# Key and query norms of a DeltaNet head in one logarithm, exponents formed once for all heads, bf16 row parts from one transpose

## The chip, the core and the metric

One core of a Trainium2 chip runs the whole program. The metric is the device time of one execution in microseconds; the time before is the median of three runs.

## The reference

A two-layer hybrid backbone over 1280 tokens (256 of context, 1024 latents on a 16 x 64 grid), width 1024. Layer 0 mixes with an mLSTM beside an S5 scan, layer 1 with a bidirectional gated DeltaNet of 8 heads of 128; each is followed by a SwiGLU network. The change lies in layer 1 alone. Cut to that:

```python
qkv = silu(depthwise_conv3x3(h @ w_in[:, :3 * 1024], conv_w))     # context: one row
q, k = l2norm(q) * 128 ** -0.5, l2norm(k)                         # per head and token
for r in (forward, backward):
    g = -exp(a_log[r]) * softplus(a_pre + dt_bias[r]);  beta = sigmoid(b_pre)
    # in chunks of 128 tokens, G = cumsum(g), Gt = its last value
    gamma = exp(G[i] - G[j]) where i >= j
    A     = strict lower of (k beta) k^T * gamma;   solve (I + A) [U, W] = [v beta, k beta exp(G)]
    attn  = q k^T * gamma;   qg = q exp(G);   kd = k exp(Gt - G)
    S     = exp(Gt) S + kd^T (U - W S);   o = qg S + attn (U - W S)
y = rmsnorm(o) * silu(z) @ w_out
```

## The kernel before

Large products run on TensorE (PE) in three parts of reduced precision (`mm3`, L116 to L118: high by high, high by low, low by high). The weights of a block come from DRAM by SP's queue; ScalarE (ACT) makes the high part (L109), GpSimd (POOL) subtracts for the low part (L110).

The projection stage of layer 1 runs over eight heads (`gdn_project`). For a head it computes keys, queries, the output gate (heads 0 to 5 here, `LATE = 6`) and values. A `conv_block` is a product in pieces of 256 and 512 tokens into PSUM, an ACT copy into a padded image (L1650, row of context L1647), the first tap on ACT (L1665, L1672), eight more taps on VectorE (DVE; L1669, each 128x1024) with two for the context row (L1674), and the silu as tanh on ACT (L1679) and a product on DVE (L1680).

Between these pieces stands a generator of side work, `gdn_keys(h)`, which is started before the values of its own head and ends during the next head. `pull` takes one piece of it halfway through each product and one after; the counts of its `yield`s (`Y1` to `Y5` = 6, 2, 1, 1, 2) set how many pieces lie between its steps. The steps are: the keys are transposed to token order (`to_tokens`, `tt_ps`, L1689) with sums of squares on ACT (L1697); the logarithm of the norms, a polynomial of small DVE operations (`log_half`, L1522 to L1536); the exponents `d_ei`, `d_ej`, `d_dx` from it and from the gates' cumulative sums `G` (L1755 to L1761); a transpose of the row exponent, `d_pr` (L1768); its split into three bf16 parts, `rows` (L1772 to L1777), which are multiplied with a selector `sel3` to spread a row over partitions (`d_pE`, L1802; `d_pe`, L1817); the queries' transposes and logarithm (L1790, L1793); the queries times their decay (POOL, L1806); and, in three groups of chunks, the decay matrices `d_e` (ACT, L1820), their sum on POOL (L1828), the key products `d_pk` (L1825) with `d_ca` (DVE, L1829), and the query products `d_pq` (L1837, DVE L1840).

PE executes in the order of the program text (`in_pe_order`). The order on DVE, ACT and POOL is set by a scheduler that models the engines; the steps of the generator carry a raised priority (`HP = 400`). After heads 3 and 6, the triangular base inverses of three heads (`gdn_base`: `b_t`, `b_x`, L1877 to L1890) are added on DVE and POOL, and the scheduler spreads them over the heads that follow. Head 7 starts its generator ahead of its queries (`last`).

Of the kernel before, what the change touches and what calls it, by code (L numbers as in the profile page):

```python
# [41 lines left out]
class Kernel:  # L42
# [77 lines left out]
    def dense(self, w, rhs, kb, n, c0=0, order=None, mid=0):  # L120
        """Feature-major product: psum[m, t] = sum_k w[k, m] act[k, t]; rhs(k) gives the two parts.
        mid: pieces of side work halfway."""
        ps = self.psd.tile([P, 512], F32, name="pd")
# [4 lines left out]
        return ps[:, :n]

    # ---------------------------------------------------------------- conditioning  # L130
    def cond_vectors(self, cp):
# [107 lines left out]
    def norm_sums(self, key, n):  # L239
        """Column sums of squares -> psum [128, n/128]."""  # L240
# [6 lines left out]
    def acts(self, ci):  # L247
        """The two parts of a chunk's activations, one after another in the same place."""
# [34 lines left out]
    # Pieces of work that follow one another while the tensor engine goes on with something else.  # L283
# [16 lines left out]
    # ---------------------------------------------------------------- program  # L300
# [43 lines left out]
    # ---------------------------------------------------------------- layer 0: mLSTM  # L344
# [26 lines left out]
    def even_select(self, c):  # L371
        """sel[p, (r, h), m] = 1 where p is row 32 r + h or 64 + 32 r + h."""
# [11 lines left out]
    def onehot(self, out, row):  # L384
        """out[p, m] = 1 where p == row."""
# [5 lines left out]
    def shift_chunks(self, dst, src, r):  # L391
        """dst[chunk] = src[previous chunk in scan order] (first chunk: 0); dims [p, c, ...]."""
# [10 lines left out]
    def mlstm_gate_rows(self, hs, gp):  # L403
        """Gate projections with their biases, a gate kind and direction to each quarter of the partitions."""
# [23 lines left out]
    def mlstm_gates(self, gk):  # L428
        """Decays, stabilisers and the factors that follow from them, in 9 pieces."""
# [12 lines left out]
        # log-sigmoid of the forget gates, order [r, c, h]  # L442
# [21 lines left out]
        # rows 32 r + h  # L464
# [35 lines left out]
        # -m in three bf16 parts: rows 0 to 63 and 64 to 127 of the first tile, rows 0 to 63 of the second  # L500
# [60 lines left out]
    def mlstm_states(self, h, t, dp, wp):  # L561
        """Scaled keys, values and the states entering each chunk, in 12 pieces."""
# [31 lines left out]
    def mlstm_weights(self, g, t, u, sp):  # L594
        """Decayed scores of a group of chunks, both directions, in 3 pieces."""
# [25 lines left out]
    def mlstm_heads(self, g, t, u, sp):  # L621
        """Normalised outputs of a group of chunks, token-major, in k + 1 pieces."""
# [38 lines left out]
    def mlstm_finish(self, g, t, u):  # L661
        """Gated outputs of a group of chunks, feature-major, in one piece."""
# [6 lines left out]
        # (tanh(o/2) + 1) * y; the factor 0.5 * head norm weight follows with the split  # L669
# [5 lines left out]
    def mlstm_outputs(self, dp, wp, sp):  # L675
        """All heads; the stages of a group of chunks lie a step apart, the states come a head ahead."""
# [38 lines left out]
    def emit(self, *streams):  # L715
        """Emit streams (generator, number of pieces), spread evenly among one another."""
# [18 lines left out]
    def run_pieces(self, *streams):  # L735
        """Emit the merged streams, the tensor engine in just this order."""
# [5 lines left out]
    def merge(streams):  # L742
        """One stream of several (generator, number of pieces), spread evenly among one another."""
# [998 lines left out]
    def gdn_keys(self, h, kqv, pool, qp):  # L1742
# [21 lines left out]
        for _ in range(Y1):  # L1764
            yield
# [567 lines left out]
```

## Time and profile before

| | us |
|---|---|
| median of three runs (lowest, highest) | 3623.36 (3621.87, 3625.25) |
| span of the profiled execution | 3623.4 |
| PE busy in the span | 3363.9 (93%) |
| DVE busy | 1981.7 (55%) |
| ACT busy | 996.8 (28%) |
| POOL busy | 1017.9 (28%) |
| projection stage of layer 1, profile time | 1850 to 2450 |

The profiled execution's own time is its span; the runs shown stand within 2 us of it. Busy time leaves out register, branch and semaphore instructions. Line numbers are those of the kernel before.

### The profile page before, as it was taken

Reading aid. Unit: us, or ns where it says so; the run is one execution under the profiler, and the core shown is the slowest. Engines: PE = TensorE matmul, PEld = TensorE weight load, DVE = VectorE, ACT = ScalarE, POOL = GpSimd, SP = SyncE. Lnnn points to the kernel's source line nnn. Section 1 sums busy time; section 2 is a strip of 40 time slices with the busy share of each in tenths; the row PEclk is TensorE's granted clock in tenths of the full one; section 3 lists DMA queues with packets and bytes.
Section 4 is the critical chain, followed back from the end, with each engine's and each line's share of the span. In section 5 each row is a group of like instructions: output and inputs, shape, how many; then the busy total and the mean of one; then the engine's idle time right before and its main releaser. Section 6 shows DMA issues by size and latency. Waiting matters only on the chain.

```text
span 3623.4 us, 48228 instructions
## 1 busy us (share of the span) xinstructions
PE 3363.9 (93%) x18527; PEld 2791.9 (77%) x18527; DVE 1981.7 (55%) x4038; ACT 996.8 (28%) x2375; POOL 1017.9 (28%) x783
## 2 busy tenths in 40 slices
PE   6998988999999999999988979778898999999999
PEld 3787767887777778888877768568897788888888
DVE  7659977434333333333489899995755432222224
ACT  3221135331111111111244535433444211111112
POOL 1011124140111111111344373644543222222123
PEclk7999989999999999999999989889999999999999
DMA  7553575512222221111123424246453011111111
GB/s 239 122 175 122 170 212 148 178 59 83 88 77 79 82 77 58 35 41 36 58 75 95 125 87 132 89 125 211 153 184 133 25 44 53 49 48 49 44 53 65
DMA packets 396828, 360.31 MB, mean 99 GB/s; under 512 B 104763, under 2 KB 329755, under 8 KB 396086
## 3 DMA queue, kind: packets, MB, share of 16 engines
q1 hardware_dynamic: 396598, 357.23, 32.3%
q8 instruction: 146, 2.39, 0.3%
q14 instruction: 84, 0.69, 0.1%
HBM read 258.92 MB, written 96.75 MB: 98 GB/s over the span
## 4 chain that ended last, share of the span: by engine, by line
PE 66%; DVE 23%; DMA 5%; issue 3%; ACT 2%; POOL 1%; SPq 1%; DVEq 0%; POOLq 0%; ACTq 0%
PE pd L116 19%; PE pd L118 18%; PE pd L117 18%; DVE d_fT L1669 4%; DVE d_qT L1669 2%; PE a_ps L181 1%; DVE s_t L1067 1%; DVE bst L1070 1%; DVE s_t L1069 1%; DVE b_x L1883 1%; DVE s_t L1068 1%; DVE b_t L1877 1%; PE e_pk L2030 1%; PE e_pu L2038 1%; DVE hl L268 1%
## 5 line engine op out<-in xcount | busy, mean ns | idle before, releaser
L116 PE MATMUL pd<-hh,w_hi 128*128 128x512 f32 (+1 forms) x3064 | 1148.8, 375 | 2.0 <-ACT hh L276 2.0
L117 PE MATMUL pd<-hl,w_hi 128*128 128x512 f32 (+1 forms) x3064 | 1134.9, 370 | 3.3 <-DVE hl L268 3.1
L118 PE MATMUL pd<-hh,w_lo 128*128 128x512 f32 (+1 forms) x3064 | 1128.2, 370 | 1.6 <-POOL w_lo L110 1.5
L110 POOL TENSOR_TENSOR w_lo<-w_raw,w_hi 128x1024 fp32r<-128x1024 f32 (+2 forms) x205 | 485.3, 2368 | 2056.8 <-ACT w_hi L109 1939.6
L116 PEld LDWEIGHTS pd<-hh,w_hi 128*128 128x128 f32 x3064 | 587.7, 192 | 114.8 <-issue 8.9
L118 PEld LDWEIGHTS pd<-hh,w_lo 128*128 128x128 f32 x3064 | 585.8, 191 | 106.4 <-issue 2.9
L117 PEld LDWEIGHTS pd<-hl,w_hi 128*128 128x128 f32 x3064 | 587.0, 192 | 103.0 <-DVE hl L268 6.1
L109 ACT CAST w_hi<-w_raw 128x1024 fp32r<-128x1024 f32 (+2 forms) x205 | 207.4, 1012 | 1012.8 <-PE pd L117 796.2
L1329 DVE SCALAR_TENSOR_TENSOR x<-pd,mod,x 128x512 f32<-128x512 f32 (+1 forms) x408 | 267.6, 670 | 267.2 <-PE pd L118 266.9
L1317 DVE TENSOR_TENSOR ntmp<-ntmp,pd 128x512 f32<-128x512 f32 (+1 forms) x110 | 69.8, 634 | 509.0 <-PE pd L118 508.8
L116 PE MATMUL pd<-g_hi,w_hi 128*128 128x512 f32 (+1 forms) x844 | 314.8, 373 | 0.6 <-DVE x L1329 0.6
L117 PE MATMUL pd<-g_lo,w_hi 128*128 128x512 f32 (+1 forms) x844 | 307.8, 365 | 0.0
L118 PE MATMUL pd<-g_hi,w_lo 128*128 128x512 f32 (+1 forms) x844 | 303.0, 365 | 0.6 <-POOL w_lo L110 0.6
L1316 DVE SCALAR_TENSOR_TENSOR ntmp<-ntmp,pd 128x512 f32<-128x512 f32 (+1 forms) x110 | 69.7, 634 | 269.9 <-ACT ntmp L1315 268.2
L1669 DVE SCALAR_TENSOR_TENSOR d_fT<-img,wcv,d_fT 128x1024 f32<-128x1024 f32 x128 | 193.7, 1513 | 22.6 <-ACT d_fT L1665 21.5
L116 PEld LDWEIGHTS pd<-g_hi,w_hi 128*128 128x128 f32 x844 | 159.5, 189 | 49.0 <-issue 21.8
L1318 ACT ACTIVATE g_hi<-ntmp 128x512 fp32r<-128x512 f32 (+1 forms) x110 | 64.7, 588 | 442.7 <-DVE ntmp L1317 442.3
L118 PEld LDWEIGHTS pd<-g_hi,w_lo 128*128 128x128 f32 x844 | 158.8, 189 | 28.9 <-issue 2.1
L117 PEld LDWEIGHTS pd<-g_lo,w_hi 128*128 128x128 f32 x844 | 159.7, 189 | 23.2
L1319 DVE SCALAR_TENSOR_TENSOR g_lo<-ntmp,g_hi 128x512 fp32r<-128x512 f32 (+1 forms) x110 | 139.6, 1269 | 68.2 <-ACT g_hi L1318 68.2
L237 POOL TENSOR_TENSOR nacc<-nacc,ntmp 128x256 f32<-128x256 f32 (+1 forms) x72 | 75.1, 1047 | 123.2 <-ACT ntmp L233 121.6
L181 PE MATMUL a_ps<-a_raw,svec 128*32 128x256 f32 x768 | 83.2, 428 | 17.9 <-DMA a_raw<-in_ada_w_dram 17.8
(550 smaller groups left out, 4767.2 us busy)
## 6 DMA issues: line engine op xcount, KB each, us to landing
w_raw<-in_ffn_w_dram SPq DMA_DIRECT2D x106, 512.0 KB
a_raw<-in_ada_w_dram SPq DMA_DIRECT2D x96, 512.0 KB
w_raw<-in_od_w_in_dram SPq DMA_DIRECT2D x32, 512.0 KB
w_raw<-in_ffn_w_dram SPq DMA_DIRECT2D x32, 384.0 KB
w_raw<-in_ev_w_in_dram SPq DMA_DIRECT2D x20, 512.0 KB
x_dr<-x SPq DMA_DIRECT2D x4, 2048.0 KB
p_dr<-mp_t SPq DMA_DIRECT2D x32, 256.0 KB
x<-x_dr SPq DMA_DIRECT2D x16, 512.0 KB
```

Of the source, the lines that this page charges most:

```text
L109: nc.scalar.copy(out=hi, in_=raw)
L110: self.w_lo_engine.tensor_tensor(out=lo, in0=raw, in1=hi.bitcast(F32), op=ALU.subtract)
L116: mm(ps, lh, rh, start=first, stop=False)
L117: mm(ps, lh, rl, start=False, stop=False)
L118: mm(ps, ll, rh, start=False, stop=last)
L181: nc.tensor.matmul(ps[32 * j:32 * j + 32, :256], self.svec[:, k], raw[:, j * 256:(j + 1) * 256], start=(k == 0), stop=(k == KB - 1), tile_ ...
L237: nc.gpsimd.tensor_tensor(out=acc, in0=acc, in1=sq, op=ALU.add)
L1316: nc.vector.scalar_tensor_tensor(out=th[:, :n], in0=th[:, :n], scalar=1.0, in1=p1, op0=ALU.add, op1=ALU.mult)
L1317: nc.vector.tensor_tensor(out=th[:, :n], in0=th[:, :n], in1=p3, op=ALU.mult)
L1319: nc.vector.scalar_tensor_tensor(out=gl[:, t0:t0 + n], in0=th[:, :n], scalar=0.5, in1=gh[:, t0:t0 + n].bitcast(F32), op0=ALU.mult, op1=ALU ...
L1329: nc.vector.scalar_tensor_tensor(out=xd, in0=ps, scalar=g, in1=xd, op0=ALU.mult, op1=ALU.add)
L1669: nc.vector.scalar_tensor_tensor(out=al, in0=g[:, dy:dy + 16, dx:dx + 64], scalar=wc(i), in1=al, op0=ALU.mult, op1=ALU.add)
```

## The change

Per head, the keys' and queries' squares go into one tile of 18 columns, with one logarithm over both; head 7, whose queries come later, takes the two separately. For this the query transposes are issued one `yield` after the key transposes, and the yields ahead of `d_pr` become one fewer. The three exponents per head are formed by one addition of 60 columns to a table `gpre`, which is made once for all heads in `gdn_gates`; the exponentials for `dg_E` and `dg_D` become one ACT operation. The row exponent is copied by ACT to three places of a zeroed 128-column tile, so that one 128x128 transpose brings it to partitions 0, 64 and 96, where the three bf16 parts are made from PSUM with four DVE operations; the selector's blocks move to the same partitions.

```diff
 # log_half(out, x, add, pool, width): its tiles are [P, width], cut to the columns of x
 # sel3: blocks at partitions 0, 64, 96 and no longer 0, 32, 64
 # gdn_gates
+        gED = gk.tile([P, 8, 2, 2, NCH], F32, name="dg_ED")
+        self.gE, self.gD = gED[:, :, 0], gED[:, :, 1]
+        self.gpre = gk.tile([P, 8, 3, 2, NCH], F32, name="dg_pre")
+        col, row, end = (self.gpre[:, :, a].rearrange("p h r c -> p r c h") for a in (0, 1, 2))
+        for r in range(2):
+            nc.vector.tensor_tensor(out=col[:, r], in0=self.lnb[:, r], in1=self.gcum[:, r], op=ALU.subtract)
+            nc.scalar.copy(out=row[:, r], in_=self.gcum[:, r])
+            nc.vector.tensor_tensor(out=end[:, r], in0=col[:, r], in1=self.gtot[:, r], op=ALU.add)
 # gdn_keys
+        def logs(sl):
+            nc.vector.tensor_scalar(out=ssq[:, sl], in0=ssq[:, sl], scalar1=0.25, scalar2=EPS, op0=ALU.mult, op1=ALU.add)
+            self.log_half(lkq[:, sl], ssq[:, sl], -0.6931471805599453, pool, NQ)
+        def factors():
+            lkb = lkq[:, ks].unsqueeze(1)
+            nc.vector.tensor_tensor(out=e3.rearrange("p a r c -> p (a r) c"), in0=self.gpre[:, h].rearrange("p a r c -> p (a r) c"),
+                                    in1=lkb.to_broadcast([P, 6, NCH]), op=ALU.add)
+            for o, n in ((0, 1), (64, 2)):
+                nc.scalar.copy(out=ei3[:, o:o + 32 * n].rearrange("p (b x) -> p b x", x=32)[:, :, :20],
+                               in_=e3[:, 1].rearrange("p r c -> p (r c)").unsqueeze(1).to_broadcast([P, n, 20]))
+            nc.scalar.activation(out=self.gED[:, h], in_=e3[:, 1:3], func=AF.Exp)
+        together = kqv[1] is not None
         with self.tc.high_priority(offset=HP):
-            self.to_tokens(kT, NCH, self.kt_dr[h], ssq, qp)
-            nc.vector.tensor_tensor(out=ej, in0=self.lnb[:, :, :, h], in1=G, op=ALU.subtract)
-            nc.vector.tensor_scalar(out=ssq, in0=ssq, scalar1=0.25, scalar2=EPS, op0=ALU.mult, op1=ALU.add)
-            self.log_half(lk, ssq, -0.6931471805599453, pool, [P, NCH])
-            nc.vector.tensor_tensor(out=ei, in0=G, in1=lkb, op=ALU.add)
-            nc.vector.tensor_tensor(out=ej, in0=ej, in1=lkb, op=ALU.add)
-            nc.vector.tensor_tensor(out=dx, in0=ej, in1=Gt, op=ALU.add)
-            nc.scalar.activation(out=self.gE[:, h], in_=ei, func=AF.Exp)
-            nc.scalar.activation(out=self.gD[:, h], in_=dx, func=AF.Exp)
-        for _ in range(Y1):
+            self.to_tokens(kT, NCH, self.kt_dr[h], ssq[:, ks], qp)
+        if together:
+            qT = kqv[1]
+            yield
+            with self.tc.high_priority(offset=HP):
+                self.to_tokens(qT, self.LCH, None, ssq[:, qs], qp)
+                logs(slice(0, NQ))
+                factors()
+                eps_factor()
+        else:
+            with self.tc.high_priority(offset=HP):
+                logs(ks)
+                factors()
+        ej = e3[:, 0]
+        for _ in range(Y1 - 1 if together else Y1):
             yield
         with self.tc.high_priority(offset=HP):
-            nc.tensor.transpose(pr[:20, :P], ei.rearrange("p r c -> p (r c)"), self.ident)
-            nc.vector.tensor_copy(rows[0:20], pr[:20, :P])
-            nc.vector.tensor_tensor(out=rem[:, 0], in0=pr[:20, :P], in1=rows[0:20], op=ALU.subtract)
-            nc.vector.tensor_copy(bb[:, 0], rem[:, 0])
-            nc.vector.tensor_copy(rows[32:52], bb[:, 0])
-            nc.vector.tensor_tensor(out=rem[:, 1], in0=rem[:, 0], in1=bb[:, 0], op=ALU.subtract)
-            nc.vector.tensor_copy(rows[64:84], rem[:, 1])
+            nc.tensor.transpose(pr, ei3, self.ident)
+            nc.vector.tensor_copy(rows, pr)
+            nc.vector.tensor_tensor(out=pr[64:128], in0=pr[64:128], in1=rows[64:128], op=ALU.subtract)
+            nc.vector.tensor_copy(rows[64:128], pr[64:128])
+            nc.vector.tensor_tensor(out=rows[96:128], in0=pr[96:128], in1=rows[96:128], op=ALU.subtract)
...
-        qT = kqv[1]
-        with self.tc.high_priority(offset=HP):
-            self.to_tokens(qT, self.LCH, None, ssq, qp)
-            nc.vector.tensor_scalar(out=ssq, in0=ssq, scalar1=0.25, scalar2=EPS, op0=ALU.mult, op1=ALU.add)
-            self.log_half(lq, ssq, 0.0, pool, [P, self.LCH])
-            nc.vector.tensor_tensor(out=lq, in0=lk[:, 2:10], in1=lq, op=ALU.subtract)
-            nc.scalar.activation(out=self.gF[:, h], in_=lq, func=AF.Exp, scale=2.0)
+        if not together:
+            qT = kqv[1]
+            with self.tc.high_priority(offset=HP):
+                self.to_tokens(qT, self.LCH, None, ssq[:, qs], qp)
+                logs(qs)
+                eps_factor()
```

Here `eps_factor` holds the last two lines of the block removed, on the columns `qs` of the one tile; the factor 0.25 in the constant that `gF` is multiplied with later becomes 0.5.

In the order of the engines this moves work at two places. On PE, in the first head, the difference from before (L1689 and L1697 are the same line of `to_tokens`; `pd` is a projection, here v's):

```order
 L117 MATMUL pd<-hl_14708,w_hi 128x256
 L118 MATMUL pd<-hh_14707,w_lo 128x256
+L1697 MATMUL tt_ps<-ident,d_qT 128x128 x8
...
-L1768 MATMUL d_pr<-ident,d_ei 20x128
+L1806 MATMUL d_pr<-ident,ei_0_15476 128x128
...
-L1689 MATMUL tt_ps<-ident,d_qT 128x128 x8
```

The query transposes move from behind `d_pr` and the next head's first key products to a place after the first twelve products of v, ahead of v's 48 wide products and of `d_pr`.

On DVE, before, behind the row parts of a head (`rows`, `d_rem`), the query logarithm (`d_ssq`, `ln_*` of 8 columns) stands between the taps of v's convolution:

```order
L1776 TENSOR_TENSOR d_rem<-d_rem,d_bb 20x128
L1777 CAST rows_0_15466<-d_rem 20x128
L1669 SCALAR_TENSOR_TENSOR d_fT<-img_15049,wcv,d_fT 128x1024
L1674 SCALAR_TENSOR_TENSOR d_fT<-row_15054,wcv,d_fT 128x256
...
L1790 TENSOR_SCALAR d_ssq<-d_ssq 128x8
...
L1522 TENSOR_SCALAR ln_m<-d_ssq 128x8
L1523 TENSOR_SCALAR ln_e<-d_ssq 128x8
```

Now (line numbers of the changed kernel; L1677 and L1688 are the taps and the silu) the one logarithm stands behind the queries' silu and ahead of the row parts, and v's taps follow those without a logarithm between them:

```order
L1688 SCALAR_TENSOR_TENSOR d_qT<-cv_th,d_qT 128x512 x2
L1716 SCALAR_TENSOR_TENSOR cv_th<-cv_th,pd 128x512 x2
L1766 TENSOR_SCALAR d_ss<-d_ss 128x18
L1522 TENSOR_SCALAR ln_m<-d_ss 128x18
...
L1536 TENSOR_TENSOR d_lkq<-ln_f,ln_p 128x18
L1771 TENSOR_TENSOR d_e_16812<-dg_pre,d_lkq 128x60
L1782 TENSOR_TENSOR d_lkq<-d_lkq 128x8
L1807 CAST rows_0_15472<-d_pr 128x128
L1808 TENSOR_TENSOR d_pr<-d_pr,rows_0_15472 64x128
L1809 CAST rows_0_15472<-d_pr 64x128
L1810 TENSOR_TENSOR rows_0_15472<-d_pr,rows_0_15472 32x128
L1677 SCALAR_TENSOR_TENSOR d_fT<-img_15049,wcv,d_fT 128x1024
```

## Rows read from the trace of the kernel before

**Rows 1.** The page, its first line and its section 1: busy time by engine.

```profile
span 3623.4 us, 48228 instructions
...
PE 3363.9 (93%) x18527; PEld 2791.9 (77%) x18527; DVE 1981.7 (55%) x4038; ACT 996.8 (28%) x2375; POOL 1017.9 (28%) x783
```

**Rows 2.** Windows by head: stretch, length, busy us per engine, clock, DMA share, GB/s.

```profile
2087.00:2177.00 90.00, 66.02 (x340) 55.82 (x339) 89.72 (x144) 33.64 (x96) 67.34 (x70) 0.85 0.27 84
...
2244.00:2309.00 65.00, 55.87 (x319) 47.19 (x318) 58.67 (x92) 34.30 (x100) 23.55 (x13) 0.94 0.40 124
...
2309.00:2394.00 85.00, 56.61 (x299) 47.32 (x299) 84.65 (x140) 32.46 (x94) 63.49 (x69) 0.84 0.24 76
```

**Rows 3.** Waits of PE, 1850 to 2450 us: total, times, longest.

```profile
PE d_pk L1825 <- DVE d_ca L1829: 21.8, 6, 8.0
...
PE d_pr L1768 <- DVE d_ej L1760: 18.0, 4, 11.7
...
PE tt_ps L1689 <- DVE d_fT L1680: 15.9, 4, 9.2
...
PE d_pq L1837 <- DVE d_ca L1829: 13.6, 2, 8.2
```

**Rows 4.** DVE by line and shape, 1850 to 2450 us: busy us, mean ns, idle before.

```profile
L1531 DVE TENSOR_SCALAR ln_f<-ln_f 128x8 f32<-128x8 f32 x8 | 10.5, 1311 | 0.0
...
L1775 DVE COPY rows<-d_bb 20x128 bf16<-20x128 bf16 x8 | 10.4, 1297 | 0.2
...
L1761 DVE TENSOR_TENSOR d_dx<-d_ej,dg_gc 128x20 f32<-128x20 f32 x8 | 4.5, 564 | 0.2
...
L1772 DVE CAST rows<-d_pr 20x128 bf16<-20x128 f32 x8 | 2.2, 276 | 4.0 <-PE d_pr L1768 3.7
...
L1523 DVE TENSOR_SCALAR ln_e<-d_ssq 128x8 int32<-128x8 int32 x8 | 1.3, 158 | 0.0
...
L1578 DVE COPY dg_t<-dg_pt 128x128 f32<-128x128 f32 x2 | 0.6, 276 | 0.0
```

**Rows 5.** Timeline of head 5 (PE, ACT, DVE): start us, us, engine, instruction, [idle before].

```profile
2248.95 0.28 PE L118 MATMUL pd<-hh,w_lo 128*128 128x256 f32 x1
...
2236.90 1.17 ACT L1665 ACTIVATE d_qT<-img,wcv 128x1024 f32<-128x1024 f32 x1
...
2240.01 1.27 DVE L1669 SCALAR_TENSOR_TENSOR d_qT<-img,wcv,d_qT 128x1024 f32<-128x1024 f32 x1
...
2243.93 9.91 DVE L1669 SCALAR_TENSOR_TENSOR d_qT<-img,wcv,d_qT 128x1024 f32<-128x1024 f32 x6
...
2254.54 1.47 DVE L1680 SCALAR_TENSOR_TENSOR d_qT<-cv_th,d_qT 128x512 f32<-128x512 f32 x2 [0.70 <-ACT cv_th L1679]
```

**Rows 6.** Timelines of DVE, POOL, ACT and PE ahead of head 5's key convolution.

```profile
2205.09 1.28 DVE L1790 TENSOR_SCALAR d_ssq<-d_ssq 128x8 f32<-128x8 f32 x1
...
2204.39 4.29 POOL L1806 TENSOR_TENSOR d_qE<-d_qE,d_qT 128x512 f32<-128x512 f32 x2 [3.80 <-ACT d_qE L1804]
...
2217.03 1.16 ACT L1679 ACTIVATE cv_th<-d_fT 128x512 f32<-128x512 f32 x2 [5.64 <-DVE d_fT L1669]
...
2223.51 1.36 DVE L1669 SCALAR_TENSOR_TENSOR d_fT<-img,wcv,d_fT 128x1024 f32<-128x1024 f32 x1 [3.75 <-ACT d_fT L1665]
...
2225.53 2.00 PE L1825 MATMUL d_pk<-d_fT 128*128 128x128 f32 x8 [1.87 <-DVE d_ca L1829]
```

**Rows 7.** A 5 us window behind a PE wait, and two PE waits in the timeline.

```profile
2142.00:2147.00 5.00, 4.68 (x15) 4.10 (x16) 5.00 (x11) 2.88 (x6) 4.19 (x6) 0.50 0.28 87
...
2142.32 2.07 PE L1837 MATMUL d_pq<-d_qT,d_fT 128*128 128x128 f32 x8 [5.44 <-DVE d_ca L1829]
...
1932.41 2.07 PE L1837 MATMUL d_pq<-d_qT,d_fT 128*128 128x128 f32 x8 [8.20 <-DVE d_ca L1829]
```

**Rows 8.** Timeline of head 6: key transposes on PE, queries' silu on DVE.

```profile
2309.05 0.69 PE L1689 MATMUL tt_ps<-ident,d_fT 128*128 128x128 f32 x2 [0.26 <-DVE d_fT L1680]
...
2322.57 1.05 DVE L1680 SCALAR_TENSOR_TENSOR d_qT<-cv_th,d_qT 128x512 f32<-128x512 f32 x1
```

More of the change, by code (lines that the diff above doesn't have):

```diff
@@ L1492, in odd_consts @@
             nc.gpsimd.memset(f, 0.0)
-            for b in range(3):
+            for b in (0, 64, 96):
                 nc.gpsimd.affine_select(out=f, in_=f, pattern=[[-1, 20], [0, P]], compare_op=ALU.not_equal,
-                                        fill=1.0, base=-32 * b, channel_multiplier=1)
+                                        fill=1.0, base=-b, channel_multiplier=1)
             nc.vector.tensor_copy(self.sel3, f)
@@ L1514, in odd_consts, with log_half @@
             tri("r64", [(a, b, not u) for a, b, u in parts])
-    def log_half(self, out, x, add, pool, shape):
+    def log_half(self, out, x, add, pool, width):
         V = self.nc.vector
-        ei = pool.tile(shape, I32, name="ln_e")
-        mi = pool.tile(shape, I32, name="ln_m")
-        a, s, p, ef = (pool.tile(shape, F32, name=f"ln_{nm}") for nm in "aspf")
+        n = x.shape[-1]
+        ei, mi = (pool.tile([P, width], I32, name=f"ln_{nm}")[:, :n] for nm in "em")
+        a, s, p, ef = (pool.tile([P, width], F32, name=f"ln_{nm}")[:, :n] for nm in "aspf")
         V.tensor_scalar(out=mi, in0=x.bitcast(I32), scalar1=0x7FFFFF, scalar2=0x3F800000, op0=ALU.bitwise_and, op1=ALU.bitwise_or)
@@ L1748, in gdn_keys @@
                 yield
-        G, Gt = self.gcum[:, :, :, h], self.gtot[:, :, :, h]
-        ei, ej, dx = (pool.tile([P, 2, NCH], F32, name=f"d_{nm}") for nm in ("ei", "ej", "dx"))
-        lk = pool.tile([P, NCH], F32, name="d_lk")
-        with self.tc.high_priority(offset=HP):
-            ssq = pool.tile([P, NCH], F32, name="d_ssk")
-            self.to_tokens(kT, NCH, self.kt_dr[h], ssq, qp)
-            nc.vector.tensor_tensor(out=ej, in0=self.lnb[:, :, :, h], in1=G, op=ALU.subtract)
-            nc.vector.tensor_scalar(out=ssq, in0=ssq, scalar1=0.25, scalar2=EPS, op0=ALU.mult, op1=ALU.add)
-            self.log_half(lk, ssq, -0.6931471805599453, pool, [P, NCH])
-            lkb = lk.unsqueeze(1).to_broadcast([P, 2, NCH])
-            nc.vector.tensor_tensor(out=ei, in0=G, in1=lkb, op=ALU.add)
-            nc.vector.tensor_tensor(out=ej, in0=ej, in1=lkb, op=ALU.add)
-            nc.vector.tensor_tensor(out=dx, in0=ej, in1=Gt, op=ALU.add)
-            nc.scalar.activation(out=self.gE[:, h], in_=ei, func=AF.Exp)
-            nc.scalar.activation(out=self.gD[:, h], in_=dx, func=AF.Exp)
@@ L1764, in gdn_keys @@
-        for _ in range(Y1):
+        NQ = NCH + self.LCH
+        e3 = pool.tile([P, 3, 2, NCH], F32, name="d_e3")
+        ssq = pool.tile([P, NQ], F32, name="d_ss")
+        lkq = pool.tile([P, NQ], F32, name="d_lkq")
+        ks, qs = slice(0, NCH), slice(NCH, NQ)
+        ei3, rows = self.ei3[h % 2], self.rows3[h % 2]
+        def logs(sl):
+            nc.vector.tensor_scalar(out=ssq[:, sl], in0=ssq[:, sl], scalar1=0.25, scalar2=EPS, op0=ALU.mult, op1=ALU.add)
+            self.log_half(lkq[:, sl], ssq[:, sl], -0.6931471805599453, pool, NQ)
@@ new lines, in eps_factor @@
+        def eps_factor():
+            lq = lkq[:, qs]
+            nc.vector.tensor_tensor(out=lq, in0=lkq[:, 2:NCH], in1=lq, op=ALU.subtract)
+            nc.scalar.activation(out=self.gF[:, h], in_=lq, func=AF.Exp, scale=2.0)
+        together = kqv[1] is not None
+        with self.tc.high_priority(offset=HP):
+            self.to_tokens(kT, NCH, self.kt_dr[h], ssq[:, ks], qp)
[11 more added lines that the diff above has]
+                factors()
@@ L1765, in gdn_keys @@
+        ej = e3[:, 0]
+        for _ in range(Y1 - 1 if together else Y1):
             yield
         with self.tc.high_priority(offset=HP):
-            pr = self.psm.tile([P, 512], F32, name="d_pr", tag="pm")
-            nc.tensor.transpose(pr[:20, :P], ei.rearrange("p r c -> p (r c)"), self.ident)
-            rows = self.rows3[h % 2]
-            rem = pool.tile([20, 2, P], F32, name="d_rem")
-            bb = pool.tile([20, 2, P], BF16, name="d_bb")
-            nc.vector.tensor_copy(rows[0:20], pr[:20, :P])
@@ L1773, in gdn_keys @@
-            nc.vector.tensor_tensor(out=rem[:, 0], in0=pr[:20, :P], in1=rows[0:20], op=ALU.subtract)
-            nc.vector.tensor_copy(bb[:, 0], rem[:, 0])
-            nc.vector.tensor_copy(rows[32:52], bb[:, 0])
-            nc.vector.tensor_tensor(out=rem[:, 1], in0=rem[:, 0], in1=bb[:, 0], op=ALU.subtract)
-            nc.vector.tensor_copy(rows[64:84], rem[:, 1])
+            pr = self.psm.tile([P, 512], F32, name="d_pr", tag="pm")[:, :P]
+            nc.tensor.transpose(pr, ei3, self.ident)
@@ L2156, in layer1 @@
                 self.rows3.append(t)
+            self.ei3 = []
+            for i in range(2):
+                t = kp.tile([P, P], F32, name=f"ei3_{i}")
+                nc.vector.memset(t, 0.0)
+                self.ei3.append(t)
             for h in range(8):
@@ L2190, in gdn_heads @@
         nc.vector.tensor_scalar(out=self.hw1, in0=self.ncols[:, 40:48], scalar1=0.5, scalar2=None, op0=ALU.mult)
-        self.nc.vector.tensor_scalar(out=self.gF, in0=self.gF, scalar1=EPS / (0.25 * 128.0 ** -0.5) ** 2, scalar2=None, op0=ALU.mult)
+        self.nc.vector.tensor_scalar(out=self.gF, in0=self.gF, scalar1=EPS / (0.5 * 128.0 ** -0.5) ** 2, scalar2=None, op0=ALU.mult)
         self.w_out = w_out = self.ins["od_w_out"][0]
```

9 lines of the change are left out of this document (3 added, 6 removed).

## The prediction

> **What bounds the kernel now.** I read the page first, then the stretches by head, then the waits of TensorE (PE), then VectorE (DVE) by line and shape, and last the timelines around one head. The page gives PE 93% busy and DVE 55% of the whole span [rows 1]; the change touches only the projection stage of the DeltaNet layer, about 1850 to 2450 us, and there the balance is another one. Head by head [rows 2]: in a plain head (head 5, 65 us) PE is busy for 55.87 and DVE for 58.67, both near their limit, and neither stops for long. In heads 3 and 6, where the base inverses of three heads are done as well, DVE is busy for 89.72 of 90 and 84.65 of 85 us: DVE alone sets the end there, and PE runs at a granted clock of 0.84 to 0.85. So a microsecond of DVE work is worth a microsecond in heads 3 and 6, and in the others only what it does to a wait of PE. Those waits are in [rows 3]: for `d_ca` ahead of `d_pk` and `d_pq` (eight waits, the longest 8.0 and 8.2 us), for the exponents ahead of `d_pr` (longest 11.7, in head 3), and for the silu of the keys ahead of their transposes (longest 9.2).
>
> **Part by part.** Prices are from this profiled execution; its span of 3623.4 us and the median of the runs, 3623.36, are the same, so the sum is taken from 3623.4.
>
> *The second logarithm.* The 8-column logarithm of the queries is 14 groups of DVE instructions, from L1531 (10.5 us for 8 heads) down to L1523 (1.3) [rows 4]; with the groups between them they come to 65.2 us, 8.1 per head. These are instructions of 8 columns: L1523 costs 158 ns, L1531 1311. They are dear because they stand in v's convolution while POOL multiplies the queries by their decay: L1790 takes 1.28 us for 8 columns beside a POOL product that runs from 2204.39 on [rows 6]. In heads 0 to 6 this work goes; eight more columns in the first logarithm are priced at nothing, since eight columns of L1523 took 158 ns and the fixed part is nearly all of that. Saved: 8.1 per head in seven heads. Head 7 starts its side work before its queries exist and keeps two logarithms.
>
> *Row parts.* Six DVE operations per head become four. The six sum to 29.7 us, from L1775 (10.4) to L1772 (2.2) [rows 4], 3.7 per head. Each of the four reads PSUM, as L1772 does (276 ns); that it now fills 128 partitions and not 20 costs nothing, for the copy L1578 of 128x128 out of PSUM takes 276 as well. Four times 0.277 is 1.1 per head; at the mean of the six (29.7/48 = 0.62) it would be 2.5. I take 1.1, the row of the same source, so 2.6 saved per head. The Trainium skill ("SBUF — State Buffer", section "Who interferes with whom") says why the two prices differ: copies and casts that enter a two-port mode, and operations with two SBUF inputs, can be shut out by a running GpSimd instruction, and one with a single SBUF input outside those modes is not. By that rule it is 1.1; against it, 2.5, and the sum would be 2 x 1.4 = 2.8 us worse; no run yet shows the new four.
>
> *Adds.* Of the four small operations that form the exponents (first L1761, 4.5 us; the four sum to 9.9, 1.2 per head) one of 60 columns stays, at 0.3. Saved 0.9. ScalarE (ACT) gets two small copies and loses one exponential per head; that lies between the log and `d_pr`, which stands 48 products of 512 columns behind the query transposes, so it is covered. The terms formed once for all heads are four additions, two ACT copies and two fills, about 1.5 us in all at the start of head 0, where PE waits for neither; without that cover they would cost those 1.5 once.
>
> So DVE loses 8.1 + 2.6 + 0.9 = **11.6 us per head** in heads 0 to 6.
>
> *The moved step.* The eight query transposes now stand on PE after twelve of v's 256-column products, and no longer behind v's 48 wide ones and `d_pr`. PE waits in line: what stands behind the transposes waits with them, all of v's projection and then its ACT evictions. No DMA moves with them (queries are not written token-major), and POOL and SP keep their order around it. In head 5 PE is at that place at 2249.2 (2248.95 plus 0.28), and the queries' silu ends on DVE at 2256.0 (2254.54 + 1.47) [rows 5]. That would be a wait of 6.9 us. Part of it closes. DVE began the keys' convolution only at 2223.51, after 3.75 idle; ACT had been late because its tanh waited 5.64 for v's convolution, the one the 8-column logarithm stretches [rows 6]. With this gone the queue moves forward until the queries' first tap meets its own input: the ACT copy of the image ends at 2238.07 (2236.90 + 1.17), 1.94 before the tap at 2240.01 [rows 5]. PE sets that time, so no more than about 2 closes: a wait of 6.9 - 2.2 = **4.7 per head**, with ACT's lag rounded in. Bounds: 6.9 if nothing closes; 2.6 if the six taps that took 9.91 in a row, 1.65 each against 1.27 for the lone one [rows 5], also lose their stretch (2.3, less a little). I take 4.7, which rests on rows alone.
>
> *The clock.* A wait of that length is followed by a slow stretch: after the 5.44 us wait that ends at 2142.32 the granted clock is 0.50, the 1.2 GHz level, for 5 us with PE busy for 4.68 [rows 7]; half of that, 2.3, is lost. Each new wait therefore costs 4.7 + 2.3 = 7.0.
>
> *The sum.* Heads 1, 2, 4, 5: +7.0 for the new wait, -1.9 for the wait of `d_pk` on `d_ca` (1.87 in [rows 6], one such in each of them), which the earlier ACT chain removes: 4 x 5.1 = +20.4. In heads 4 and 5 the products behind that wait run at the slow clock (eight in 2.00 us [rows 6]), which gives back 1.0 each: -2.0. Head 0: +7.0, less its 8.20 wait of `d_pq` [rows 7], ahead of which 8.1 us of DVE work goes, less 2.3 of clock: -3.5. Heads 3 and 6: DVE sets the end, -11.6 each, -23.2; the wait of PE for the queries is long there (in head 6 the key transposes end at 2309.74 and the queries at 2323.62 [rows 8]) but DVE fills it with base work that must be done anyway. Head 7: row parts and adds only, 3.5, of which about half lies ahead of a PE wait: -2. Together 20.4 - 2.0 - 3.5 - 23.2 - 2.0 = -10.3, so **3613 us**.
>
> **Rivals.** *The query wait rules (slower).* If the keys' convolution starts no earlier, each of heads 0, 1, 2, 4, 5 waits 6.9 and loses 2.3 of clock, and `d_pk` keeps its waits: 5 x 9.2 = 46, less head 0's 10.5, less 23.2, less 2: +10.3, **3634**. It decides from a mean wait of about 6 us upward. For it: key and query convolutions follow each other on DVE without a gap from 2240 to 2254 [rows 5]. Against it: the 3.75 idle before them [rows 6]. Chance 0.18.
>
> *The wait does not open.* If a lighter DVE also runs its taps unstretched and the silu overtakes PE, the five waits are gone: -10.3 - 35 = -45, **3578**. Against it: ACT's image copy ends 11.2 us before PE reaches the place, and eight taps at 1.27 with the two halves of the silu need more. Chance 0.10.
>
> *Half of heads 3 and 6 given back (no change).* There PE stands for some 12 us behind the query transposes, with v's projection behind it. If DVE runs out of base work meanwhile, PE's delay returns as DVE idle time later. Half the saving of these heads lost, 11.6: +1.3, **3624 to 3625**. The same time results if the removed operations were mostly filling time that POOL's lock leaves idle, so that the change does not do what it says. For it: DVE has almost no idle time to absorb anything [rows 2]. Chance 0.22.
>
> **The numbers.** The forecast has 0.50, with a range of its own of 3601 to 3624. 0.2% of the span, about what a measurement of this kernel can tell from no change, is 7.2 us, so faster is under 3616 and slower over 3631. Faster: 0.40 of the forecast, all of the second rival and 0.05 of the third, 0.55; same: 0.10, and 0.15 of the third, 0.25; slower: the first rival and 0.02 of the third, 0.20. The range 3595 to 3635 takes in the first and third rivals' values and leaves out the second and the tail of the first.
>
> **What would show it.** In the changed profile: no 8-column log instructions outside head 7; four row operations near 0.28 us; a new PE wait of 4 to 5 us for `d_qT` ahead of its transposes in heads 0, 1, 2, 4, 5, with a clock near 0.5 behind it; waits of `d_pk` for `d_ca` gone in the plain heads; heads 3 and 6 shorter by about 11. The sum is wrong if the query waits are over 6 or absent, if heads 3 and 6 do not shorten though DVE is lighter, or if PE waits longer than before for `d_pr`.

## The result and the profile after

The changed kernel takes 3661.54 us (median of four runs, 3659.54 to 3665.96) against 3624.31 us for the kernel before beside it: a ratio of 1.0104, 95% interval 1.0092 to 1.0116. It is 37 us **slower**; forecast were 3613, and a range of 3595 to 3635. The profiled execution has a span of 3664.2, 40.8 over that of before, so the sums below are made against 40.8; it is the slowest of the four, so some 4 us of the 40.8 are its own.

The page of the changed kernel, first line and busy time:

```profile
span 3664.2 us, 48092 instructions
...
PE 3381.0 (92%) x18527; PEld 2806.9 (77%) x18527; DVE 1955.5 (53%) x3892; ACT 1000.3 (27%) x2385; POOL 1021.3 (28%) x783
```

PE is busy a little longer than before and DVE a little less: 1955.5 against 1981.7 us, [rows 1]. The forecast took 11.6 us off DVE in each of seven heads, 81 in all; 26 are gone.

The projection stage by windows (columns as in [rows 2]), first that of before as a whole, then the changed kernel: the whole stage, a plain head (from the transposes of head 4's queries to those of head 5's), and five microseconds behind the wait of head 5. The last two are head 3 in both kernels, from the first DVE tap of its queries to that of the next head's:

```profile
1850.00:2450.00 600.00, 504.03 (x2737) 423.51 (x2736) 552.29 (x850) 273.98 (x774) 294.66 (x234) 0.92 0.35 106
```

```profile
1850.00:2490.00 640.00, 518.20 (x2740) 435.68 (x2739) 533.72 (x710) 278.70 (x787) 300.21 (x234) 0.90 0.32 98
...
2212.00:2284.00 72.00, 62.90 (x347) 53.11 (x347) 54.29 (x67) 33.46 (x93) 23.81 (x11) 0.95 0.33 105
...
2284.00:2289.00 5.00, 4.83 (x24) 4.65 (x25) 2.41 (x6) 4.75 (x24) 0.00 (x0) 0.60 0.28 105
```

```profile
2083.00:2172.90 89.90, 65.92 (x340) 55.73 (x339) 89.62 (x145) 33.90 (x97) 68.44 (x71) 0.85 0.28 88
```

```profile
2098.80:2192.80 94.00, 67.39 (x339) 56.97 (x338) 92.74 (x132) 33.73 (x97) 67.73 (x71) 0.85 0.30 88
```

The stage is 40 us longer, 640 against 600, and what follows it is as long as before (3664.2 - 2490 and 3623.4 - 2450 agree to 1 us). PE's busy time in it rose by 14.2 (504.03 to 518.20), about what the slower clock makes of it (504.03 x 0.92 / 0.90 = 515, an estimate), and its idle time by the other 26. Head 3 is not shorter but 4 us longer, and DVE is busy for 92.74 of its 94 us, where 11.6 were to go. A plain head takes 72 us where it took 65, and DVE is now busy for only 54.29 of them.

Length of each head in us, from the first DVE tap of its queries to that of the next head's (head 7 up to the first product of the next stage, `e_pp`):

| head | 0 | 1 | 2 | 3 | 4 | 5 | 6 | 7 |
|---|---|---|---|---|---|---|---|---|
| before | 87.2 | 65.6 | 64.1 | 89.8 | 67.1 | 64.8 | 84.8 | 61.2 |
| changed | 85.3 | 72.0 | 71.8 | 94.0 | 76.1 | 71.9 | 91.5 | 60.8 |
| forecast change | -3.5 | +5.1 | +5.1 | -11.6 | +4.1 | +4.1 | -11.6 | -2.0 |

Heads 1 to 6 are all longer. Another 3.6 us of the profile lie ahead of head 0's first tap.

Waits of PE in the stage (total, times, longest), the answer to [rows 3]:

```profile
PE tt_ps L1697 <- DVE d_qT L1688: 45.6, 6, 9.2
...
PE d_pk L1854 <- DVE d_ca L1858: 23.0, 8, 7.8
...
PE d_pr L1806 <- ACT ei L1775: 7.9, 3, 4.4
...
PE d_pE L1831 <- DVE rows L1810: 5.6, 2, 3.6
...
PE d_pq L1866 <- DVE d_ca L1858: 2.9, 1, 2.9
```

The new wait, for `d_qT` ahead of the query transposes, is there six times, in heads 1 to 6, 6.5 to 9.2 us each (7.69 in head 5); head 0 has none. Those of `d_pr` and `d_pq` fell from 18.0 and 13.6 to 7.9 and 2.9; with the smaller ones the net is 26 more. Behind the new wait of head 5 the clock is 0.60 over five microseconds (the third window), as [rows 7] let one expect.

Head 5 again, with the instructions of [rows 5] and [rows 6], in order of time (L1687 is the tanh, L1673 the first tap on ACT, L1677 the taps on DVE, L1688 the silu, L1697 the transposes):

```profile
2245.66 1.15 ACT L1687 ACTIVATE cv_th<-d_fT 128x512 f32<-128x512 f32 x2 [4.54 <-DVE d_fT L1677]
...
2250.79 1.21 ACT L1673 ACTIVATE d_fT<-img,wcv 128x1024 f32<-128x1024 f32 x1
...
2252.04 1.38 DVE L1677 SCALAR_TENSOR_TENSOR d_fT<-img,wcv,d_fT 128x1024 f32<-128x1024 f32 x1 [4.08 <-ACT d_fT L1673]
...
2264.14 1.17 ACT L1673 ACTIVATE d_qT<-img,wcv 128x1024 f32<-128x1024 f32 x1
...
2268.93 1.28 DVE L1677 SCALAR_TENSOR_TENSOR d_qT<-img,wcv,d_qT 128x1024 f32<-128x1024 f32 x1
...
2272.86 9.87 DVE L1677 SCALAR_TENSOR_TENSOR d_qT<-img,wcv,d_qT 128x1024 f32<-128x1024 f32 x6
...
2273.79 1.25 PE L1697 MATMUL tt_ps<-ident,d_fT 128*128 128x128 f32 x10
...
2283.42 1.47 DVE L1688 SCALAR_TENSOR_TENSOR d_qT<-cv_th,d_qT 128x512 f32<-128x512 f32 x2 [0.69 <-ACT cv_th L1687]
...
2284.17 1.97 PE L1697 MATMUL tt_ps<-ident,d_qT 128*128 128x128 f32 x8 [7.69 <-DVE d_qT L1688]
...
2301.95 1.86 DVE L1677 SCALAR_TENSOR_TENSOR d_fT<-img,wcv,d_fT 128x1024 f32<-128x1024 f32 x1 [1.16 <-ACT d_fT L1673]
```

The silu of the queries starts on DVE at 2283.42, its first half lets PE go on at 2284.17, and PE had stood there for 7.69 us. The idle time of DVE ahead of the keys' first tap, whose end was to close a part of the wait, is still there, 4.08 us, and was 3.75 before [rows 6]: ACT's first tap for the keys stands behind the tanh of v, and that waited 4.54 for v's convolution. But v's convolution begins with v's image, and v's projection now stands on PE behind the query transposes: after these started at 2284.17, the first tap of v on DVE comes at 2301.95, 17.8 us later. This closes a **ring**: queries' silu (DVE), transposes and projection of v (PE), image (ACT), convolutions of v, next k, next q (DVE, one after another), queries' silu. Its length is what a plain head now takes: 17.8 us from the transposes to v's first tap, in which DVE has the logarithm and the row parts to do and otherwise stands, and then some 54 us of taps, silus and the waits between them until the queries are ready again. Of the 72 us DVE is idle for 17.7 and PE for 9.1 (72.00 - 62.90): neither is full, and each waits for a part of the ring in which others work.

### The profile page after: what moved, and what is told of

The parts are those of the page before. It is cut to its first block, busy times and chain, and to the rows that moved or that the text cites. A ratio compares the mean times of both kernels' runs of the same rounds, so it can differ in the third digit from the quotient of the medians.

```text
span 3664.2 us, 48092 instructions
## 1 busy us (share of the span) xinstructions
PE 3381.0 (92%) x18527; PEld 2806.9 (77%) x18527; DVE 1955.5 (53%) x3892; ACT 1000.3 (27%) x2385; POOL 1021.3 (28%) x783
## 4 chain that ended last, share of the span: by engine, by line
PE 64%; DVE 22%; DMA 5%; issue 4%; ACT 3%; POOL 1%; SPq 1%; DVEq 0%; POOLq 0%; ACTq 0%
PE pd L116 18%; PE pd L117 18%; PE pd L118 18%; DVE d_fT L1677 4%; DVE d_qT L1677 2%; PE a_ps L181 1%; DVE bst L1070 1%; DVE s_t L1067 1%; DVE b_x L1912 1%; DVE b_t L1906 1%; DVE s_t L1069 1%; DVE s_t L1068 1%; PE e_pk L2059 1%; DMA a_raw<-in_ada_w_dram 1%; PE e_pu L2067 1%
## 5 line engine op out<-in xcount | busy, mean ns | idle before, releaser
L110 POOL TENSOR_TENSOR w_lo<-w_raw,w_hi 128x1024 fp32r<-128x1024 f32 (+2 forms) x205 | 478.6, 2335 | 2075.2 <-ACT w_hi L109 2021.7
L1317 DVE TENSOR_TENSOR ntmp<-ntmp,pd 128x512 f32<-128x512 f32 (+1 forms) x110 | 69.7, 634 | 508.3 <-PE pd L118 508.1
L1677 DVE SCALAR_TENSOR_TENSOR d_fT<-img,wcv,d_fT 128x1024 f32<-128x1024 f32 x128 | 216.3, 1690 | 27.2 <-ACT d_fT L1673 24.9
L1316 DVE SCALAR_TENSOR_TENSOR ntmp<-ntmp,pd 128x512 f32<-128x512 f32 (+1 forms) x110 | 69.7, 633 | 270.0 <-ACT ntmp L1315 268.2
```

Of the source, the lines that this page charges most:

```text
L110: self.w_lo_engine.tensor_tensor(out=lo, in0=raw, in1=hi.bitcast(F32), op=ALU.subtract)
L1316: nc.vector.scalar_tensor_tensor(out=th[:, :n], in0=th[:, :n], scalar=1.0, in1=p1, op0=ALU.add, op1=ALU.mult)
L1317: nc.vector.tensor_tensor(out=th[:, :n], in0=th[:, :n], in1=p3, op=ALU.mult)
L1677: nc.vector.scalar_tensor_tensor(out=al, in0=g[:, dy:dy + 16, dx:dx + 64], scalar=wc(i), in1=al, op0=ALU.mult, op1=ALU.add)
```

## The experiments

Ratios are to the kernel before on the same chip, with their 95% intervals; medians in us. In the short diffs a minus is the changed kernel, unless the kernel before is named.

**Which part costs.** Run x1_two_logs undoes the joint logarithm and the move, run x2_early_only does the move alone, in the kernel before.

```diff
-        together = kqv[1] is not None
+        together = False
```

> The changed kernel with two logarithms and the query transposes in their old place; row parts and joint exponents stay. Theory A (a ring: PE waits for the queries' silu, v's projection stands behind that wait, and the convolutions of v, k and q follow one another on DVE behind v's projection): the waits for d_qT are gone and the time is that of the kernel before or a little less, 3612 to 3626 us. Rival B (the row parts in PSUM, the ACT copies ahead of d_pr or the new order on DVE cost the time): it stays above 3645.

Measured: 3621.84, ratio 0.9988 (0.9979 to 0.9998).

```diff
 # the kernel before, gdn_keys, behind the logarithm and exponentials of the keys
-        for _ in range(Y1):
+        if early:                       # heads 0 to 6
+            yield
+            self.to_tokens(kqv[1], self.LCH, None, ssq, qp)
+        for _ in range(Y1 - 1 if early else Y1):
             yield
```

> The kernel before with one edit: in heads 0 to 6 the query transposes and their squares stand one piece behind the key transposes; both logarithms, exponents and row parts as before. Theory A: waits for d_qT of 6 to 9 us in heads 1 to 6 and a time of 3655 to 3675 us, at least that of the changed kernel, since no DVE work is saved. Rival B: under 3635.

Measured: 3671.92, ratio 1.0128 (1.0113 to 1.0143). Waits of PE in these two, first x1_two_logs, which has none for `d_qT`, then x2_early_only:

```profile
PE d_pr L1806 <- ACT ei L1775: 24.0, 7, 12.1
...
PE d_pk L1854 <- DVE d_ca L1858: 23.3, 8, 7.9
...
PE d_pq L1866 <- DVE d_ca L1858: 11.3, 2, 6.0
```

```profile
PE tt_ps L1689 <- DVE d_qT L1680: 41.3, 7, 9.2
...
PE d_pE L1809 <- DVE rows L1783: 20.7, 2, 11.1
```

So the move alone costs 46.5 us and no less than the whole change; row parts and joint exponents cost nothing. Theory A stands against rival B. By the ratios the whole change takes 9 us less than the move alone (1.0128 - 1.0104), but the two intervals touch, and the waits for `d_qT` are smaller in the move alone (41.3 against 45.6). What it has more of is the wait of `d_pE` for the row parts in heads 3 and 6, 20.7 us against 5.6. That the saving on DVE counts for something inside the ring is not shown by these two.

**Is it a ring?** A ring gives back any time that is taken out of its DVE part, in every head. Both kernels lose two of the eight taps of the queries' convolution (that part of the computation is left out):

```diff
-            if i != 4:
+            if i != 4 and not (off == 0 and i in (0, 8)):
```

> The changed kernel with two of the eight VectorE taps of the queries' convolution left out. Theory A (ring): each of the six waits for d_qT becomes shorter by the two taps, 2.5 to 3.3 us, so 15 to 22 us less than the changed kernel, 3640 to 3647 us. Rival C (the waits for d_qT only take the place of idle time that PE would have anyway, and the time is set elsewhere): less than 8 us below the changed kernel.

> The kernel before with the same two taps left out. Theory A: no ring, so only heads 3 and 6, where VectorE is busy throughout, and head 7 give something: 5 to 11 us below the kernel before, 3613 to 3620 us, half of what the changed kernel gives. Rival C: as much as the changed kernel gives, in both.

Measured: in the changed kernel 3642.31, ratio 1.0051 (1.0036 to 1.0066), 19.2 us less than it took; in the kernel before 3616.24, ratio 0.9971 (0.9961 to 0.9981), 9.5 less. The waits for `d_qT` in x6_after_6taps:

```profile
PE tt_ps L1697 <- DVE d_qT L1688: 27.5, 6, 5.2
```

They came down from 45.6 to 27.5, 3.0 per wait, about two taps (they average 1.40 us). By the medians the cut is worth twice as much in the changed kernel as in the one before; rival C is out. In which heads the kernel before gains is not shown: the profiled execution of x7_before_6taps is the slowest of its nine, 1.4 us below that of before.

**Moving the transposes back, with one logarithm.** Three kernels keep the joint logarithm and put the query transposes later among the pieces of side work:

```diff
 # x4_a3b3: pieces ahead of the query transposes, and from there to d_pr
-            yield                                            # 1, then Y1 - 1 = 5
+            for _ in range(3): yield                         # 3, then 3
 # x3_a4b4: 4, then 4, and none (Y2) behind d_pr
 # x5_a4b4y3: as x3_a4b4, and Y3 + 2 pieces ahead of d_pE
```

> The changed kernel with the query transposes three pieces behind the key transposes (it was one) and three ahead of d_pr: PE reaches them 12 products of 0.12 us and 12 of 0.23 later, 4.2 us. Theory A: waits of 6.5 to 9.2 become 2.3 to 5.0, about 4 us and some clock less in six heads: 3630 to 3640 us. Rival B: 3655 or more, as the changed kernel.

> The changed kernel with the query transposes four pieces behind the key transposes, d_pr four behind these (where the query transposes of the kernel before stood) and no piece between d_pr and what follows: PE reaches the transposes 6.9 us later. Theory A: waits for d_qT of 0 to 2.3 us, 3605 to 3625 us, if the row parts are ready for d_pE; if they are not, a new wait ahead of d_pE of 1 to 3 us per head and 3620 to 3640. Rival B: 3650 or more.

> As x3_a4b4, with two more pieces ahead of the queries' decay products d_pE. Theory A: the waits for the row parts (3.2 us in plain heads) go too, and nothing of the ring is left: 3608 to 3622 us. If the row parts simply move with VectorE's queue, the waits stay and it is 3630 or more.

Measured: 3646.66 (1.0061; 1.0044 to 1.0078), 3638.59 (1.0038; 1.0025 to 1.0051) and 3629.30 (1.0012; 1.0002 to 1.0021). PE's waits in x4_a3b3, x3_a4b4 and x5_a4b4y3, in this order:

```profile
PE tt_ps L1697 <- DVE d_qT L1688: 25.8, 7, 9.4
```

```profile
PE d_pE L1832 <- DVE rows L1811: 31.3, 7, 7.2
...
PE tt_ps L1697 <- DVE d_qT L1688: 1.4, 2, 1.0
```

```profile
PE d_pr L1807 <- ACT ei L1775: 22.1, 4, 11.2
...
PE tt_ps L1697 <- DVE d_qT L1688: 2.6, 4, 1.6
```

The wait for `d_qT` falls with each step, 45.6, 25.8, 1.4, as the ring says, and so does the time; x4_a3b3 is 7 us above what was expected of it, and one of its waits, behind head 3, is still 9.4. In x3_a4b4 the wait is gone and another has its place: the row parts now come after d_pr's later transpose, and `d_pE` waits 31.3 us for them, the case that was named. With two more pieces that one goes too (x5_a4b4y3), yet the time stays 0.1% above the kernel before: 3608 to 3622 was expected. So one logarithm instead of two brings nothing even where the waits for `d_qT` are nearly gone (those of `d_pr`, 22.1 us, are about as long as the 18.0 and 1.0 of before). That left the other half of the sum to be explained.

**What the second logarithm is worth.** First its place, with two logarithms and the query one where GpSimd (POOL) was to run no decay product:

```diff
+            logs(ks); factors()
+            for _ in range(4): yield
+            self.to_tokens(qT, self.LCH, None, ssq[:, qs], qp); logs(qs); eps_factor()
+            # then Y1 - 4 pieces and d_pr
```

> The changed kernel with two logarithms: that of the keys at once, the query transposes and their 8-column logarithm four pieces behind the key transposes, ahead of d_pr, where no decay product runs on GpSimd. Theory A: the queries are ready when PE comes, and the 8-column logarithm takes about 2.3 us instead of 8.1: 5 to 6 us of VectorE work less in heads 3 and 6 than in x1_two_logs, 3603 to 3615 us. Against it: where PE still waits 2 us or more per head for d_qT, 3620 to 3630.

Measured: 3630.81, ratio 1.0016 (1.0006 to 1.0025), just above the range of the case against it, though the waits for `d_qT` are a little shorter than its 2 us per head: 9.4 us in five heads, 1.9 each (the line below). Nor did the 8-column logarithm become cheap: its 14 groups take 41.1 us, 5.1 per head, against 65.2 in the kernel before, where 2.3 per head was expected. It now stands often beside the part of the base inverses that POOL does.

```profile
PE tt_ps L1698 <- DVE d_qT L1689: 9.4, 5, 3.9
```

Then the kernel before without the queries' logarithm at all; the norm of the queries is left out of the computation:

```diff
-            self.log_half(lq, ssq, 0.0, pool, [P, self.LCH])
-            nc.vector.tensor_tensor(out=lq, in0=lk[:, 2:10], in1=lq, op=ALU.subtract)
+            nc.vector.tensor_tensor(out=lq, in0=lk[:, 2:10], in1=ssq, op=ALU.subtract)
```

> The kernel before without the 13 groups of the queries' logarithm (55.7 us of VectorE by the rows of the kernel before, 7 per head); nothing is moved. Theory D (most of that is waiting for a running GpSimd instruction, and whatever VectorE instruction stands there next waits in its place): VectorE's busy time falls by 15 to 30 us only, the taps of v and k get longer (1513 ns before), and the time is 2 to 9 us less, 3616 to 3623. Rival E (the durations are work, as the prediction took them): VectorE's busy time falls by 50 or more and heads 3 and 6 by 7 each, 3603 to 3611 us.

Measured: 3615.92, ratio 0.9970 (0.9956 to 0.9984), 9.8 us less. Page and taps of y4_no_qlog:

```profile
PE 3367.9 (93%) x18518; PEld 2796.6 (77%) x18527; DVE 1960.3 (54%) x3918; ACT 997.0 (28%) x2375; POOL 1023.1 (28%) x783
```

```profile
L1669 DVE SCALAR_TENSOR_TENSOR d_fT<-img,wcv,d_fT 128x1024 f32<-128x1024 f32 x128 | 199.0, 1555 | 25.7 <-ACT d_fT L1665 24.2
```

DVE's busy time fell by 21.4 us (1981.7 to 1960.3), where the removed rows had come to 55.7; the taps of k and v grew from 1513 ns to 1555. Heads 3 and 6 are only 1.8 and 0.4 us shorter by the marks of the table above, where rival E had 7 each. Theory D stands, but not all of the difference was handed on. The records of successive DVE instructions overlap at their ends (L1790 of [rows 6] ends at 2206.37, and the next tap starts at 2206.28), so a sum of rows is more than the engine's time: by their start and end times only 37.0 of the 55.7 us are covered by the removed instructions alone. Of these 37.0, 15.6 went to other instructions and 21.4 were saved.

The gain in time, 9.8 us, is just beyond the 2 to 9 that were expected, and not all of it was open to the change. In the profiles head 7 falls from 61.2 to 54.8 us, 6.4 of the 15 us that the eight heads lose (the span is 9 us shorter): in the kernel before, PE waits there for the logarithm (the line below, its waits), and the change leaves head 7 its two logarithms.

```profile
PE d_pk L1825 <- DVE ln_s L1530: 5.1, 1, 5.1
```

**The two small parts, each alone in the kernel before.** Run y1_rows_only has the ACT copies, the 128x128 transpose and the four operations; run y2_exponents_only the table, the one addition and the one exponential.

```diff
 # y1_rows_only
-            nc.tensor.transpose(pr[:20, :P], ei.rearrange("p r c -> p (r c)"), self.ident)
+            nc.tensor.transpose(pr, ei3, self.ident)      # and the four operations of the change
 # y2_exponents_only
-            nc.vector.tensor_tensor(out=ei, in0=G, in1=lkb, op=ALU.add)      # and d_ej, d_dx
+            nc.vector.tensor_tensor(out=e3, in0=gpre[:, h], in1=lkb, op=ALU.add)
```

> The kernel before with the row parts alone made the new way (ACT copies, one 128x128 transpose, four operations from PSUM). Theory D: the stretch of L1775 and L1777 goes to the taps behind them; 0 to 4 us less than before. Rival E: 2.6 us less in each of heads 3, 6 and 7, 5 to 8 us less.

> The kernel before with the exponents alone formed the new way (one table, one addition of 60 columns, one exponential); two logarithms, six row operations. Theories D and E alike: 0.9 us of VectorE per head, 0 to 3 us less than before.

Measured: 3625.68 and 3624.66, both 0.9997 (0.9988 to 1.0007 and 0.9988 to 1.0006): no change. The taps of k and v in y1_rows_only, and the copy L1775 of before (here L1809) in y2_exponents_only:

```profile
L1669 DVE SCALAR_TENSOR_TENSOR d_fT<-img,wcv,d_fT 128x1024 f32<-128x1024 f32 x128 | 205.6, 1606 | 26.9 <-ACT d_fT L1665 25.9
```

```profile
L1809 DVE COPY rows<-d_bb 20x128 bf16<-20x128 bf16 x8 | 16.8, 2097 | 0.3
```

In the first the stretch has gone from L1775 to the taps (1606 ns against 1513); DVE is busy for 13.3 us less (1981.7 to 1968.4), and the time is the same. In the second nothing was done to this copy, and it takes 2097 ns where it took 1297 [rows 4]. Its eight times show why: it takes 2.2 to 2.4 us beside POOL's subtraction for the low part of the weights (L110), four times in the kernel before and seven times here, and 0.18 us where no POOL instruction runs.

**Once more.** x1_two_logs had seemed ahead by 0.12%.

> The kernel of x1_two_logs once more, for whether its lead of 0.12% over the kernel before is one. By the runs of y1_rows_only and y2_exponents_only (0.03% each) the lead is 0 to 0.1%: 3621 to 3626 us. If row parts and exponents help each other, 0.1 to 0.2%.

Measured: 3625.15, ratio 0.9999 (0.9990 to 1.0008). It is no faster than the kernel before, and none of the versions that compute the whole reference is clearly so.

## Why the prediction was wrong

**The step that failed on the sign** is in the moved step: "Part of it closes." The wait itself was found (6.9 us by [rows 5], whose numbers give 6.8; measured 7.69 in that head), and it was said that v's projection stands behind it. It was not followed on: v's image, v's convolution and with it the tanh ahead of the keys' first tap come later by just that wait, so the keys cannot start earlier relative to PE, and the 3.75 us do not close. The price was 6.5 to 9.2 a head where 4.7 was taken and 6.9 was the bound; five of the six waits pass even the bound. The new waits are 45.6 us in all; forecast were 23.5, in five heads. PE's busy time rose by 2.4 per wait (14.2 over six), where 2.3 was taken for the clock, so that term held.

**The step that cost most** is "Heads 3 and 6: DVE sets the end, -11.6 each". They became 4.2 and 6.7 us longer, 34 of the 51 us by which the profile (3664.2) misses the sum. It had two things wrong. The new wait costs time there too: it is 7.25 us long in head 3 and 7.33 in head 6. And a DVE that is busy for 89.62 of 89.90 us was taken for the limit, though much of what fills it, the base operations, can move: the 64 of head 3 run from first to last over 106.6 us in the kernel before and over 77.7 in the changed one. With DVE lighter by 21.4 us in all (y4_no_qlog) and by 13.3 (y1_rows_only), head 3 was shorter by only 1.8 and 2.1 us, head 6 by 0.4 and 0.1. What does set the length of these heads in the kernel before stays open; the longest wait of PE in head 3 is the one for `d_pr`, 11.7 [rows 3]. Two of the prediction's own signs of being wrong came: query waits over 6, and heads 3 and 6 that do not shorten.

**The step that failed on the size of the saving** is the 11.6 us of DVE per head, taken as work. The durations of the 8-column instructions, and of L1775 and L1777, were read rightly, also that they were dear because of a POOL instruction; from this it should have followed that the instruction that stands there next pays the same. (The 8.1 per head are a mean that takes in 12.2 of head 7; heads 0 to 6 have 7.6.) In the changed kernel the four row operations take what was forecast, and the wide logarithm is cheap. The line groups of DVE in the changed kernel:

```profile
L1677 DVE SCALAR_TENSOR_TENSOR d_fT<-img,wcv,d_fT 128x1024 f32<-128x1024 f32 x128 | 216.3, 1690 | 27.2 <-ACT d_fT L1673 24.9
...
L1531 DVE TENSOR_SCALAR ln_f<-ln_f 128x18 f32<-128x18 f32 x7 | 1.5, 219 | 0.0
...
L1807 DVE CAST rows<-d_pr 128x128 bf16<-128x128 f32 x8 | 2.3, 288 | 35.1 <-PE d_pr L1806 35.1
...
L1808 DVE TENSOR_TENSOR d_pr<-d_pr,rows 64x128 f32<-64x128 f32 x8 | 2.5, 309 | 0.3
```

But the taps of k and v went from 193.7 us to 216.3, and the base operations grew as well. First these of the changed kernel, then taps and base operations of the kernel before, by line over all shapes (columns as in [rows 4]):

```profile
L1912 DVE TENSOR_TENSOR b_x<-b_x,b_t 128x30 f32<-128x30 f32 (+14 forms) x60 | 36.5, 609 | 0.9
...
L1906 DVE TENSOR_TENSOR b_t<-b_x 128x30 f32<-128x30 f32 (+14 forms) x60 | 33.2, 553 | 0.8
```

```profile
L1669 DVE SCALAR_TENSOR_TENSOR d_fT<-img,wcv,d_fT 128x1024 f32<-128x1024 f32 x128 | 193.7, 1513 | 22.6 <-ACT d_fT L1665 21.5
...
L1883 DVE TENSOR_TENSOR b_x<-b_x,b_t 128x30 f32<-128x30 f32 (+14 forms) x60 | 28.2, 471 | 0.3
...
L1877 DVE TENSOR_TENSOR b_t<-b_x 128x30 f32<-128x30 f32 (+14 forms) x60 | 25.0, 416 | 0.2
```

That is 22.6 and 16.5 us (53.2 to 69.7) returned, while the context row's taps, the queries' silu and the narrow `d_ca` fell by 10 together. The Trainium skill ("SBUF — State Buffer", "Who interferes with whom") has the rule for it: a DVE operation with two SBUF inputs is shut out while a GpSimd instruction that reads SBUF runs. Taps and base sums are such operations, and the trace agrees: a tap of k or v that starts while a POOL instruction runs takes 2.07 us on average in the changed kernel, any other 1.28, and 66 of the 128 do so, where 54 did before. The sum used this rule for the new four operations alone, and did not ask what would stand beside GpSimd in place of the old ones. Only the third rival did, with operations that "were mostly filling time"; it shared a chance of 0.22 and gave back half of heads 3 and 6, where all of it was gone. The overlap of records takes its share as well: over the whole trace the durations of DVE add up to 53.7 us less than before, and its busy time is 26.2 less.

**What came as forecast.** No 8-column logarithm outside head 7; the row operations at 0.28 to 0.31 us, forecast 0.28; `d_pk` waits for `d_ca` in plain heads 0.7 instead of about 1.9, though not gone; a slow clock behind each new wait (0.57 to 0.67 over five microseconds); the exponents and the ACT copies without a visible cost. The first rival named the mechanism of the loss and its sign, at 3634; it let heads 3 and 6 keep 23 us of gain that do not exist, and counted no wait in them. Without these 23 its sum would be 3657, and the measured profile 3664.

## What to carry to other kernels

Before a transpose or product is moved forward on an engine that works in order, follow what stands behind it all the way round: if that feeds the engine the new wait is for, a ring is closed, and the period is then the sum of its parts (here 72 us, with PE busy for 62.90 and DVE for 54.29). A duration that is stretched by another engine's instruction is in part a wait; removing the instruction can hand the wait to the next one, so price what is removed at its unstretched time (here 158 ns [rows 4] to 219 ns for a small operation; the 120 instructions of y4_no_qlog come to 19 to 26 us by that, an estimate, and 21.4 were saved) and check it by the engine's busy time. An engine that is busy throughout a stretch need not set its end: where work that can wait fills it, look for what shortens the stretch when the engine gets lighter. Here 13.3 us less DVE time changed nothing.

## What the runs showed that was not expected

Leaving out a logarithm whose rows sum to 55.7 us took 21.4 us off the engine's busy time, and a copy of 20x128 that no edit had touched went from 1297 to 2097 ns on average because that POOL subtraction held it up seven times instead of four. An operation of 128 columns that reads its value from PSUM and writes its result back in place (L1808, 309 ns) costs hardly more than the cast from PSUM to SBUF (L1807, 288 ns).
